# A hybrid SSD and pooling trunk on one core: the gate tiles of the first layer projected ahead of the scans in seven-product pairs, one convolution for prompt and sample rows, and another tail

## The chip, the cores and the metric

The kernel runs on one core of a Trainium2 chip. The metric is the device time of one execution in microseconds (us). Two times matter here: the timed runs (their median is the figure for the kernel) and one profiled execution, which left the profile that is read below. TensorE is called PE in the profile, its weight loads PEld, VectorE is DVE, ScalarE is ACT, GpSimd is POOL, and SyncE, which issues the DMAs, is SP.

## The reference

One inference step of a two-layer trunk runs over 1,024 prompt tokens of one sequence and over 8 sample sequences of 8 new tokens each, which come with states. Both layers are normed and modulated by a conditioning vector, and both add their output to x. All data are float32.

```python
# layer 0: Mamba-2 SSD
zxbcdt = h @ w_in                      # 1024 -> 2048 gates z, 4096 x/B/C, 32 dt
conv = conv_b + sum(xp[:, k:k + L] * conv_w[k] for k in range(4))   # causal, 3 rows of state ahead
xbc_act = silu(conv)
dt = softplus(dt_raw + dt_bias)
y, new_ssm = ssd_scan(xs, dt, A, Bm, Cm, ssm_prev)   # chunks of 128 tokens, 32 heads in 8 groups
gated = (y + d_skip * xs) * silu(z)
out = (groupwise_rmsnorm(gated) * norm_g) @ w_out    # 2048 -> 1024
# layer 1: causal pooling
uz = h @ w_in                          # 1024 -> 2048 u, 2048 z
pooled_g = window_mean(u_g, w) - u_g   # four channel groups, w = 2, 4, 8, 16
out = (grouped_matmul(pooled) * ch_scale * silu(z)) @ w_out
# then y = rmsnorm(x, final_norm_g); the new states are outputs too
```

## The kernel before: tiles, stages and order

Channels lie on the 128 partitions and tokens in the free dimension: 1,088 columns, of which 1,024 are the prompt and 64 the samples. A projection tile is 128 output channels. Its columns are done in three chunks (CH: 364, 364, 360). Float32 accuracy comes from two-part operands: each factor is rounded to a high part and the rest is a low part, and `mm1` (lines 158 to 163) issues three matmuls, high by high, high by low, low by high. A tile of the first layer is so 8 steps of the contraction x 3 chunks x 3 = 72 matmuls. A weight tile comes by DMA and is split by ScalarE (line 118) and VectorE (line 119).

The stages in order of time:

- `setup` and `front` load x, compute the norm and the modulated input hn (high and low parts, 8 tiles), and meanwhile the first two tiles and the 32 columns of dt. The modulation's shift reaches dt by 64 small matmuls of their own (pds).
- The first layer has 8 groups of 4 heads. A group needs 6 projection tiles in the order B, C, x, x, z, z. `proj_group` does them in units of one chunk (24 matmuls, 4 us). B, C and x tiles go through `conv_tile`: GpSimd does the first of four steps, VectorE the other three, prompt and sample columns in separate instructions, then tanh on ScalarE and a last step on VectorE. The two z tiles are gated (`proj_chunk`) and stay on the chip.
- `scan_group(g)` runs the scan of group g over 8 prompt chunks and one sample step. `ssd_layer` weaves it with the projections of group g + 1: one step of the scan, then one or two units, by a list of counts; the rest of the previous scan comes behind the first unit. The scan of group 7 is woven with the output projection (`op_units`).
- `ssd_out` finishes the output projection, norms and modulates for the second layer.
- `pool_layer` projects u and z: two pairs of tiles plainly, then 14 pairs (`fast_pairs`) with seven half-size products instead of eight. A pair of tiles with two halves of the contraction and two halves of the columns is a 2 x 2 block product; the seven products need sums of weight blocks (`w_sums`, GpSimd) and of activation blocks (`act_sums`, VectorE and ScalarE, called T1 to T4), and additions of the results on VectorE. A product is 24 matmuls of 272 columns. Then come the window sums (`u_pool`), the group matmuls (`pool_mix`) and the output projection.
- `last_part` does the last output tiles in column chunks (END: 416, 416, 256), and `done` and `scale` norm and store each chunk.

The order of instructions on each engine comes from the order of the code as priorities; a scheduler at build time may move a ready instruction ahead of an earlier one that is not ready by its own costs. Tiles come from `Slots` (31 buffers of 1,088 columns) or from pools with a fixed number of buffers: three PSUM tiles (mm) for the projections, two `raw` tiles for the convolution, two high and two low weight tiles. All DMAs are issued in order by SP.

## Time and profile before

| what | value |
|---|---|
| timed runs | 1692.45, 1697.51, 1698.06 us; median 1697.51 |
| profiled execution | 1692.15 us |
| its span, first to last instruction | 1690.4 us |
| mean granted TensorE clock | 0.993 |
| PE, PEld, DVE, ACT, POOL busy | 98, 93, 73, 43, 34% |
| HBM read, written | 160.95, 46.84 MB |

Stages of the span: the first layer's projections and scans from 70 to about 880 us, its output projection to 1030, the second layer's plain pairs to 1087, its fast pairs to 1382, the group matmuls to 1486, and the output projection and the tail to the end.

How to read the rows: in a group's row the numbers behind the bar are the busy time of the group in us, the mean ns of one instruction, and the idle time of the engine just ahead of them with what ended most of it. A matmul's own duration includes its latency, and matmuls overlap: 364 columns take about 330 ns each, but start 166 ns apart, so rates are worked out from counts in a stretch of time. For the same reason PE counts as busy in short pauses. In the timeline a row has the start, the length, the instruction, how many were merged, and in brackets how long its engine had been idle and what released it.

### The profile page before, as it was taken

To read this page: it belongs to the slowest core of one execution; us is meant where nothing else is said; L and a number is where in the kernel's file an instruction comes from. 1 tells how busy PE (TensorE), PEld (TensorE's weight loads), DVE (VectorE), ACT (ScalarE), POOL (GpSimd) and SP (SyncE) were. 2 spreads that over 40 slices of the span, in tenths; PEclk is the share of its full clock that TensorE was granted. 3 is DMA by queue.
4 is the path that set the end of the run, shared out by engine and by line. 5 is a ranking of instruction groups with operands and counts; after the bars stand their busy time and mean duration, and the time that the engine had idled before them with its cause. 6 is when DMAs were issued, how large, how long until landed. Compare 5 with 4: busy or idle time off the path is not lost.

```text
span 1690.4 us, 29827 instructions
## 1 busy us (share of the span) xinstructions
PE 1659.3 (98%) x11701; PEld 1579.5 (93%) x11701; DVE 1230.0 (73%) x2157; ACT 732.2 (43%) x1498; POOL 569.8 (34%) x600
## 2 busy tenths in 40 slices
PE   8999999999999999999999999999999999999997
PEld 6899999999999999998889998999999999999996
DVE  6776767677676767687788447988899996555546
ACT  5435554655555555656542027533333333221123
POOL 0224435353544445262320022365566630000012
PEclk9999999999999999999999999999999999999998
DMA  9222242333334142415874132133323368511102
GB/s 355 83 75 83 91 152 86 130 101 129 97 115 138 50 132 72 156 48 170 299 250 184 38 116 80 67 127 108 110 96 109 108 234 328 174 50 51 38 26 106
DMA packets 104461, 209.72 MB, mean 124 GB/s; under 512 B 16225, under 2 KB 56321, under 8 KB 104321
## 3 DMA queue, kind: packets, MB, share of 16 engines
q1 hardware_dynamic: 104320, 207.82, 35.9%
q8 instruction: 92, 1.51, 0.4%
q14 instruction: 49, 0.39, 0.1%
HBM read 160.95 MB, written 46.84 MB: 123 GB/s over the span
## 4 chain that ended last, share of the span: by engine, by line
PE 83%; DVE 9%; DMA 3%; issue 2%; ACT 2%; POOL 1%; SPq 0%; DVEq 0%; ACTq 0%; POOLq 0%
PE mm L161 19%; PE mm L162 18%; PE mm L163 18%; PE st L911 5%; PE st L909 5%; PE st L910 5%; PE y L549 2%; PE S L558 2%; DVE ws L771 2%; PE am L236 1%; PE y L553 1%; PE tr L499 1%; PE tr L495 1%; DVE xbc L325 1%; DMA ada<-adaA 1%
## 5 line engine op out<-in xcount | busy, mean ns | idle before, releaser
L161 PE MATMUL mm<-hh,wh 128*128 128x364 f32 (+1 forms) x1104 | 366.4, 332 | 0.0
L163 PE MATMUL mm<-hh,wl 128*128 128x364 f32 (+1 forms) x1104 | 363.6, 329 | 0.0
L162 PE MATMUL mm<-hl,wh 128*128 128x364 f32 (+1 forms) x1104 | 363.5, 329 | 0.0
L161 PE MATMUL mm<-gh,wh 128*128 128x364 f32 (+3 forms) x768 | 253.6, 330 | 3.7 <-DVE gs L698 2.6
L163 PE MATMUL mm<-gh,wl 128*128 128x364 f32 (+3 forms) x768 | 253.4, 330 | 0.0
L162 PE MATMUL mm<-gl,wh 128*128 128x364 f32 (+3 forms) x768 | 252.8, 329 | 0.0
L118 ACT ACTIVATE wh<-wr 128x1024 fp32r<-128x1024 f32 (+1 forms) x97 | 95.8, 987 | 284.1 <-PE mm L162 260.3
L695 DVE SCALAR_TENSOR_TENSOR x<-mm,gat,x 128x364 f32<-128x364 f32 (+3 forms) x192 | 108.9, 571 | 146.5 <-PE mm L163 145.9
L161 PEld LDWEIGHTS mm<-hh,wh 128*128 128x128 f32 x1104 | 208.1, 188 | 4.0 <-issue 2.8
L162 PEld LDWEIGHTS mm<-hl,wh 128*128 128x128 f32 x1104 | 208.0, 188 | 1.3 <-issue 1.0
L163 PEld LDWEIGHTS mm<-hh,wl 128*128 128x128 f32 x1104 | 207.9, 188 | 0.8 <-issue 0.4
L325 DVE SCALAR_TENSOR_TENSOR xbc<-raw,cwh,xbc 128x1024 f32<-128x1024 f32 x96 | 138.8, 1446 | 31.0 <-POOL xbc L322 31.0
L161 PEld LDWEIGHTS mm<-gh,wh 128*128 128x128 f32 x768 | 144.9, 189 | 6.6 <-issue 3.6
L163 PEld LDWEIGHTS mm<-gh,wl 128*128 128x128 f32 x768 | 144.9, 189 | 0.7 <-issue 0.5
L162 PEld LDWEIGHTS mm<-gl,wh 128*128 128x128 f32 x768 | 144.8, 189 | 0.7 <-issue 0.6
L711 POOL TENSOR_TENSOR ss<-ss,sq 128x364 f32<-128x364 f32 (+1 forms) x24 | 25.7, 1070 | 352.7 <-ACT sq L710 352.7
L911 PE MATMUL st<-hh,w 128*128 128x272 f32 x448 | 129.3, 289 | 0.0
L909 PE MATMUL st<-hh,w 128*128 128x272 f32 x448 | 129.1, 288 | 0.0
L910 PE MATMUL st<-hl,w 128*128 128x272 f32 x448 | 128.8, 288 | 0.0
L534 POOL TENSOR_TENSOR ea<-xbc,ea 128x512 f32<-128x512 f32 x56 | 83.1, 1484 | 119.7 <-ACT ea L493 112.3
L119 DVE TENSOR_TENSOR wl<-wr,wh 128x1024 fp32r<-128x1024 f32 (+1 forms) x97 | 110.9, 1143 | 13.7 <-ACT wh L118 13.3
L506 ACT ACTIVATE M<-acb,tkac 128x128 f32<-128x128 f32 x256 | 91.9, 393 | 25.9 <-PE y L549 25.2
(279 smaller groups left out, 3890.3 us busy)
## 6 DMA issues: line engine op xcount, KB each, us to landing
wr<-win SPq DMA_DIRECT2D x48, 512.0 KB, 4.1
acb<-acd SPq DMA_DIRECT2D x64, 256.0 KB, 3.7
wr<-pin SPq DMA_DIRECT2D x32, 512.0 KB, 3.7
x<-xT SPq DMA_DIRECT2D x16, 544.0 KB, 7.7
gyd<-xbc SPq DMA_DIRECT2D x16, 544.0 KB, 2.7
gr<-gyd SPq DMA_DIRECT2D x16, 544.0 KB, 6.8
zgd<-pz SPq DMA_DIRECT2D x16, 544.0 KB, 2.7
pld<-pl SPq DMA_DIRECT2D x16, 544.0 KB, 2.8
```

The source lines that it names most:

```text
L118: self.nc.scalar.activation(hi[:, :nk, :], raw[:, :nk, :], AF.Copy)
L119: self.nc.vector.tensor_tensor(out=lo[:, :nk, :], in0=raw[:, :nk, :], in1=hi[:, :nk, :].bitcast(F32), op=ALU.subtract)
L161: nc.tensor.matmul(ps[:, :n], hi[:, k, :], ah[:, a:a + n], start=first, stop=False)
L162: nc.tensor.matmul(ps[:, :n], hi[:, k, :], al[:, a:a + n], start=False, stop=False)
L163: nc.tensor.matmul(ps[:, :n], lo[:, k, :], ah[:, a:a + n], start=False, stop=last)
L325: nc.vector.scalar_tensor_tensor(out=dst[:, :NP], in0=raw[:, k:k + NP], scalar=w[k], in1=dst[:, :NP], op0=ALU.mult, op1=ALU.add)
L506: nc.scalar.activation(M[:L, r, :L], acb[:L, r, :], AF.Relu, bias=tk["ac", cc][:L, col + r:col + r + 1], scale=-1.0)
L534: nc.gpsimd.tensor_tensor(out=ea, in0=C[:, tok].unsqueeze(1).to_broadcast([P, 4, 128]), in1=ea, op=ALU.mult)
L695: nc.vector.scalar_tensor_tensor(out=x[d][:, a:a + pn], in0=ps[:, :pn], scalar=self.gat[l][:, d, 8:9], in1=x[d][:, a:a + pn], op0=ALU.mult ...
L909: nc.tensor.matmul(ps[c][:, :QUART], hi[:, k], xh[:, t], start=(k == 0), stop=False)
L910: nc.tensor.matmul(ps[c][:, :QUART], hi[:, k], xl[:, t], start=False, stop=False)
L911: nc.tensor.matmul(ps[c][:, :QUART], lo[:, k], xh[:, t], start=False, stop=(k == 3))
```

## The change

- The gate (z) tiles of all groups are projected ahead of the scans. Tiles 0 and 1 (group 0's gates) run in the front beside the modulation, in place of B and C; tiles of group 1 follow plainly; the twelve others, in six pairs, and group 0's B, C pair and x pair go through seven products (`FRONT`, `front_pairs`, `fast_pair`). The activation sums are made from x (`act_sums_front`), which therefore gets the shift added by one more pass of ScalarE; dt is then computed from that x, and the pds matmuls go. T1 overwrites half of hn, which is stored to DRAM (`b12d`) first and loaded back after the last product that needs T1.
- Each gate tile is stored to DRAM (`zsd`) and loaded again in the scan of its group, at chunk 6 (`load_z`).
- The groups' projections from group 1 on are four tiles (12 units); the weave has one unit a step.
- The convolution runs over 1,112 contiguous columns that hold prompt and sample rows with their states. Its first step is on ScalarE, with an accumulator of its own; `raw` has three buffers. The last step is split in two.
- The scan's small tiles lie in a pool that takes the place of the front's pool. There are 30 slots, 4 more in the front, and 7 wide ones later.
- The second layer takes its channel groups in the order of windows 4, 8, 16, 2, and loads and splits its group weights two tiles at a time.
- In the tail the norm of a chunk comes behind one or two units of the next chunk, the last chunk's squares are all summed by TensorE, the reciprocal root is written to PSUM too and read there by VectorE, and the shares of GpSimd and the order of the stores are others.

The core of the diff (`product`, the 24 matmuls of one product, is the old inner function of `fast_pairs` made a method; `fast_pairs` now calls `fast_pair`):

```diff
-WINDOWS = (2, 4, 8, 16)
+GROUPS = (1, 2, 3, 0)
+WINDOWS = tuple(2 << g for g in GROUPS)
...
-PK = (0, 2)
-OUT = (((0, 1), (2, 3), (4, 5), (6, 7)), ((0, 1), (2, 3), (4, 5), (6, 7)), ((0, 1), (2, 3, 4), (5, 6, 7)))
-NSLOT_A = 31
-NSLOT_B = 6
+PK = (2, 4, 3)
+OUT = (((0, 1), (2, 3), (4, 5), (6, 7)), ((0, 1), (2, 3), (4, 5), (6, 7)), ((5, 6, 7), (3, 4), (0, 1, 2)))
+NSLOT_A = 30
+NSLOT_B = 7
+NSLOT_E = 4
+FRONT = (("z", 2), ("z", 3), ("z", 4), ("z", 5), ("b", 0), ("z", 6), ("x", 0), ("z", 7))
...
+            nc.scalar.activation(t[:, :pn], t[:, :pn], AF.Identity, bias=sh)
...
     def conv_tile(self, ti, raw, dst, ncv):
-        nc = self.nc
+        nc, n = self.nc, 1112
         rv = raw[:, 1027:1115].rearrange("p (b w) -> p b w", w=11)
-        dv = dst[:, NP:TOK].rearrange("p (b i) -> p b i", i=8)
         w = [self.cwh[:, 4 * ti + k:4 * ti + k + 1] for k in range(4)]
-        b = self.cwh[:, 128 + ti:129 + ti]
-        nc.gpsimd.tensor_scalar(dst[:, :NP], raw[:, 0:NP], w[0], b, op0=ALU.mult, op1=ALU.add)
-        nc.gpsimd.tensor_scalar(dv, rv[:, :, 0:8], w[0], b, op0=ALU.mult, op1=ALU.add)
+        acc = self.raw_tile()
+        nc.scalar.activation(acc[:, :n], raw[:, :n], AF.Identity, bias=self.cwh[:, 128 + ti:129 + ti], scale=w[0])
         for k in range(1, 4):
-            nc.vector.scalar_tensor_tensor(out=dst[:, :NP], in0=raw[:, k:k + NP], scalar=w[k], in1=dst[:, :NP], op0=ALU.mult, op1=ALU.add)
-            nc.vector.scalar_tensor_tensor(out=dv, in0=rv[:, :, k:k + 8], scalar=w[k], in1=dv, op0=ALU.mult, op1=ALU.add)
+            nc.vector.scalar_tensor_tensor(out=acc[:, :n], in0=raw[:, k:k + n], scalar=w[k], in1=acc[:, :n], op0=ALU.mult, op1=ALU.add)
         nc.gpsimd.tensor_copy(ncv[:, 0:1, :], raw[:, 1024:1027].unsqueeze(1))
         nc.gpsimd.tensor_copy(ncv[:, 1:9, :], rv[:, :, 8:11])
-        th = raw[:, :TOK]
-        nc.scalar.activation(th, dst, AF.Tanh)
-        nc.vector.scalar_tensor_tensor(out=dst, in0=th, scalar=1.0, in1=dst, op0=ALU.add, op1=ALU.mult)
+        nc.scalar.activation(raw[:, :n], acc[:, :n], AF.Tanh)
+        nc.vector.scalar_tensor_tensor(out=dst[:, :NP], in0=raw[:, :NP], scalar=1.0, in1=acc[:, :NP], op0=ALU.add, op1=ALU.mult)
+        th, v = (t[:, 1027:1115].rearrange("p (b w) -> p b w", w=11)[:, :, 0:8] for t in (raw, acc))
+        nc.vector.scalar_tensor_tensor(out=dst[:, NP:TOK].rearrange("p (b i) -> p b i", i=8), in0=th, scalar=1.0, in1=v, op0=ALU.add, op1=ALU.mult)
+    def raw_tile(self):
+        return self.gp.tile([P, 1115], F32, tag="raw", bufs=3, name=self.name("raw"))
...
+    def gate_chunk(self, dst, c, ps):
+        self.z_chunk(dst, ps[:, :CH[c][1]], *CH[c])
+    def gate_store(self, i, dst):
+        self.nc.sync.dma_start(self.zsd[i], dst)
+        self.slots.free(dst)
...
+        def load_z():
+            for q in range(2):
+                zs.append(self.slots.get("z"))
+                nc.sync.dma_start(zs[q], self.zsd[2 * g + q])
...
+            if c == 6:
+                load_z()
...
+        self.last_sq = []
         for c, (a, n) in enumerate(chunks):
             for w, d in zip(ws, range(8 - nt, 8)):
+                if l and c and d == 8 - nt + c:
+                    done(c - 1)
                 self.op_unit(l, x, d, w, acts, (a, n))
                 if l == 0:
                     nc.sync.dma_start(self.x1d[d][:, a:a + n], x[d][:, a:a + n])
-                if l and c == 2 and d == 7:
-                    t = self.mt.tile([P, 416], F32, tag="mt", bufs=2, name=self.name("sq"))
+                if l and c == 2:
+                    t = self.slots.get("sq")
                     nc.scalar.activation(t[:, :n], x[d][:, a:a + n], AF.Square)
-                    self.last_sq = t
+                    self.last_sq.append(t)
                 else:
                     self.sq_add(ss, x[d], d, False, a, n, nc.vector)
                 if c == 2 and d % 2 and nt == 4:
                     self.stream_split(self.wpos + d // 2 - 2)
-            done(c)
+            if l == 0 or c == 2:
+                done(c)
...
+    def fast_pair(self, u, z, after):
+        nc, product = self.nc, self.product
+        def add(out, x, y):
+            nc.vector.tensor_tensor(out=out, in0=x, in1=y, op=ALU.add)
+        def put(dst, half, c, x, y):
+            t, o, rv = dst
+            o += HALF * half + QUART * c
+            n = QUART - NS if rv is not None and half and c else QUART
+            add(t[:, o:o + n], x[:, :n], y[:, :n])
+            if n < QUART:
+                add(rv, *(v[:, n:].rearrange("p (b i) -> p b i", i=8) for v in (x, y)))
+        cs = [slice(QUART * c, QUART * c + QUART) for c in range(2)]
+        s = self.tp.tile([P, HALF], F32, tag="mt2", bufs=2, name=self.name("u2"))
+        z1 = z[0][:, z[1]:z[1] + HALF]
+        ps = product(("mm", "mm"), "B11")
+        for c in range(2):
+            nc.scalar.activation(s[:, cs[c]], ps[c], AF.Copy)
+        after("B11")
+        ps = product(("tr", "tr"), "B21")
+        for c in range(2):
+            put(u, 0, c, ps[c], s[:, cs[c]])
+        after("B21")
+        ps = product(("y", "y"), "T2")
+        for c in range(2):
+            add(s[:, cs[c]], ps[c], s[:, cs[c]])
+        after("T2")
+        ps = product(("mm", "S"), "T3")
+        for c in range(2):
+            add(z1[:, cs[c]], ps[c], s[:, cs[c]])
+        after("T3")
+        ps = product(("mm", "mm"), "T1")
+        for c in range(2):
+            add(s[:, cs[c]], ps[c], s[:, cs[c]])
+            put(z, 1, c, ps[c], z1[:, cs[c]])
+            after(f"z1{c}")
+        after("T1")
+        ps = product(("tr", "tr"), "T4")
+        for c in range(2):
+            put(z, 0, c, ps[c], z1[:, cs[c]])
+            after(f"z0{c}")
+        after("T4")
+        ps = product(("y", "y"), "B22")
+        for c in range(2):
+            put(u, 1, c, ps[c], s[:, cs[c]])
+        after("B22")
...
         items = []
-        for g in range(8):
-            for ii in range(6):
+        items += [(io["win"][i], 8) for i in (4, 5, 10, 11)]
+        items += [(io["win"][6 * g + {"b": 0, "x": 2, "z": 4}[kind] + i], 0) for kind, g in FRONT for i in range(2)]
+        for g in range(1, 8):
+            for ii in range(4):
...
-        pds = self.pp.tile([P, 512], F32, tag="tr", bufs=2, name="pds")
-        for k in range(8):
-            for j in range(4):
-                nc.tensor.matmul(pds[32 * j:32 * j + 32, :9], wdt[:, k, :], self.shf[0][:, k, :], start=k == 0, stop=k == 7, tile_position=(0, 32 * j))
         sl.free(rst, wdts, *self.wslots)
-        dt = self.dt_phase(pdt, pds)
+        dt = self.dt_phase(pdt)
         next(dt)
         for i in range(2):
+            dst = sl.get("z")
             for c in range(3):
-                self.proj_chunk(G, i, c, pst[i][c])
-        for i, _ in enumerate(self.proj_group(G, 2)):
-            if i > 5:
-                next(dt, None)
+                self.gate_chunk(dst, c, pst[i][c])
+            self.gate_store(i, dst)
+        ops = self.act_sums_front()
+        for i in range(2):
+            w, dst = self.stream_next(), sl.get("z")
+            for c, ch in enumerate(CH):
+                ps = self.mm_tile()
+                self.mm3(ps, w, self.hn, ch)
+                self.gate_chunk(dst, c, ps)
+                next(ops)
+            self.gate_store(2 + i, dst)
+        self.front_pairs(ops, dt)
...
+    def act_sums_front(self):
+        nc, sl, x = self.nc, self.slots, self.xs
+        h1, h2 = slice(0, HALF), slice(HALF, TOK)
+        self.T = {}
+        def sub(out, x, y):
+            nc.vector.tensor_tensor(out=out, in0=x, in1=y, op=ALU.subtract)
+        def split(x, hi, lo):
+            nc.scalar.activation(hi, x, AF.Copy)
+            nc.vector.tensor_tensor(out=lo, in0=x, in1=hi.bitcast(F32), op=ALU.subtract)
+        def new(i, k, x):
+            self.T[i, k] = t = sl.get("t", F32R, extra=i < 4)
+            split(x, t[:, h1], t[:, h2])
+        for k in range(4):
+            p, r = x[k], x[k + 4]
+            sub(p[:, h1], p[:, h2], p[:, h1])
+            sub(p[:, h2], r[:, h2], p[:, h2])
+            sub(r[:, h2], r[:, h2], p[:, h1])
+            new(2, k, r[:, h2])
+            for i in range(2):
+                nc.sync.dma_start(self.b12d[2 * k + i], self.hn[k][i][:, h2].bitcast(F32))
+            yield
+        for k in range(4):
+            new(3, k, x[k][:, h2])
+            if k % 2:
+                yield
+        for k in range(4):
+            split(x[k][:, h1], self.hn[k][0][:, h2], self.hn[k][1][:, h2])
+            sl.free(x[k])
+        yield
+        for k in range(4):
+            r = x[k + 4]
+            sub(r[:, h1], r[:, h1], r[:, h2])
+            new(4, k, r[:, h1])
+            sl.free(r)
+        yield
+    def front_pairs(self, ops, dt):
+        nc, sl = self.nc, self.slots
+        self.fast_init(len(FRONT))
+        G = None
+        for n, (kind, g) in enumerate(FRONT):
+            if kind == "z":
+                ts = [sl.get("z") for _ in range(2)]
+                outs = [(t, 0, None) for t in ts]
+            else:
+                G = G or self.proj_open(g)
+                ii = 2 * (kind == "x")
+                ts = [self.proj_begin(G, ii + i) for i in range(2)]
+                outs = [(t, 3, t[:, 1027:1115].rearrange("p (b w) -> p b w", w=11)[:, :, 3:11]) for t in ts]
+            def after(x):
+                if kind == "z" and x[0] == "z":
+                    a = HALF * int(x[1]) + QUART * int(x[2])
+                    self.z_chunk(ts[1], ts[1][:, a:a + QUART], a, QUART)
+                elif kind == "z" and x in ("B21", "B22"):
+                    for c in range(2):
+                        a = HALF * (x == "B22") + QUART * c
+                        self.z_chunk(ts[0], ts[0][:, a:a + QUART], a, QUART)
+                    if x == "B22":
+                        self.gate_store(2 * g, ts[0])
+                elif kind == "z" and x == "T4":
+                    self.gate_store(2 * g + 1, ts[1])
+                if kind != "z" and x == "B22":
+                    for i in range(2):
+                        self.proj_end(G, ii + i, ts[i])
+                if n == 0 and x in ("B11", "B21"):
+                    next(ops)
+                if 0 < n < 3 and x in ("B21", "T3", "T4"):
+                    next(dt, None)
+                if n == len(FRONT) - 1:
+                    if x in ("T2", "T3"):
+                        sl.free(*[self.T[int(x[1]), k] for k in range(4)])
+                    elif x == "T1":
+                        for k in range(4):
+                            for i in range(2):
+                                nc.sync.dma_start(self.hn[k][i][:, HALF:].bitcast(F32), self.b12d[2 * k + i])
+            self.fast_pair(*outs, after)
+        sl.free(*[self.T[4, k] for k in range(4)])
...
-                self.weave(itertools.islice(sc, 11), pr, (1, 2, 2, 2, 2, 2, 2, 2, 1, 1, 1))
+                self.weave(itertools.islice(sc, 11), pr, (1, 1, 1, 1, 1, 1, 1, 1, 1, 1, 2))
...
-        self.weave(itertools.islice(sc, 10), itertools.islice(pr, 15), (1, 2, 2, 2, 2, 2, 1, 1, 1, 1), False)
+        self.weave(itertools.islice(sc, 10), itertools.islice(pr, 10), (1,), False)
...
-                self.ms_log(ss, rst, a, n, 1.0 / 1024, 0, more=self.last_sq if c == 2 else None)
+                ps = self.ms_log(ss, rst, a, n, 1.0 / 1024, 0, more=self.last_sq if c == 2 else None)
+                nc.scalar.activation(ps[:, :n], rst[:, a:a + n], AF.Exp, scale=-0.5)
                 self.rstd(rst[:, a:a + n])
-            if c:
-                scale(c - 1)
+            norms.append(ps)
+            if c == 0:
+                scale(0)
             if c == 2:
-                scale(c)
+                scale(1)
+                scale(2)
+        norms = []
```

244 lines of the change are left out of this document (108 added, 136 removed).

## The prediction

> **What bounds the kernel now.** I read the page first, then the windows by stage, the groups of instructions, the waits of TensorE, and the timeline around its longest stall in the scans.
>
> ```profile
> span 1690.4 us, 29827 instructions
> PE 1659.3 (98%) x11701; PEld 1579.5 (93%) x11701; DVE 1230.0 (73%) x2157; ACT 732.2 (43%) x1498; POOL 569.8 (34%) x600
> PE 83%; DVE 9%; DMA 3%; issue 2%; ACT 2%; POOL 1%; SPq 0%; DVEq 0%; ACTq 0%; POOLq 0%
> ```
>
> The matmuls fill the span and carry 83% of the chain that ended last, so only fewer or cheaper matmuls, or the removal of TensorE's few idle stretches, can shorten it. How full the other engines are in each stage says what can take TensorE's place. The next answer has, for each stretch, busy time and count of each engine, then clock, DMA share and GB/s.
>
> ```profile
> core 0: us, PE busy (x) PEld busy (x) DVE busy (x) ACT busy (x) POOL busy (x), PEclk, DMA share, GB/s
> 40.00:60.00 20.00, 20.00 (x174) 16.07 (x173) 15.26 (x34) 8.17 (x14) 0.00 (x0) 1.00 0.36 123
> 340.19:437.74 97.55, 97.55 (x723) 90.78 (x726) 69.56 (x125) 54.29 (x128) 43.41 (x50) 1.00 0.34 113
> 773.00:776.00 3.00, 3.00 (x17) 2.72 (x17) 1.01 (x1) 2.61 (x7) 0.32 (x1) 0.61 0.22 91
> 840.00:880.00 40.00, 40.00 (x344) 33.74 (x343) 37.24 (x72) 20.71 (x42) 10.01 (x7) 1.00 0.72 248
> 1030.00:1087.00 57.00, 53.42 (x311) 50.91 (x310) 54.22 (x108) 40.18 (x91) 13.41 (x23) 1.00 0.13 41
> 1100.00:1380.00 280.00, 280.00 (x2233) 279.97 (x2232) 247.89 (x396) 90.41 (x173) 166.48 (x131) 1.00 0.34 117
> 1382.00:1486.00 104.00, 100.22 (x601) 99.11 (x600) 68.64 (x99) 34.22 (x40) 2.16 (x2) 1.00 0.68 245
> 1500.00:1640.00 140.00, 140.00 (x845) 140.00 (x845) 69.48 (x137) 22.42 (x22) 1.93 (x2) 1.00 0.12 41
> ```
>
> One group of the first layer (a scan woven with the next group's six projection tiles) takes 97.55 us, and TensorE has no gap in it. The second layer's seven-product pairs (1100 to 1380) keep TensorE full although VectorE is at 89%.
>
> **The products.** Dense 364-column matmuls take 140/845 = 0.166 us each, the 272-column ones of a seven-product pair 280/2233 = 0.1254 us. A plain pair of tiles is 2 x 24 x 3 = 144 matmuls, 23.9 us; a fast pair is 7 x 24 = 168, 21.1 us. Eight pairs change form, six of gates and two of group 0's B, C and x: 8 x 2.8 = **-22.7 us**. This is the main term. The Trainium skill ("TensorE: Matmul & The Clock Gate", Back-to-back issue gap) gives N/2.4 + 2.5 ns; by it the eight pairs would save about 21 us, an estimate from that page. The two rows are 8% dearer, and they decide.
>
> **The front.** The 64 small pds matmuls go. The modulate gets one more ScalarE pass over 1,024 columns for each of eight tiles, because x must now hold the shifted value for the sums; it is like the pass of L303.
>
> ```profile
> 69.54 0.80 PE L1117 MATMUL pds<-shf,wdt 128*32 128x9 f32 x64
> L303 ACT ACTIVATE hh<-x,shf 128x1024 fp32r<-128x1024 f32 (+2 forms) x10 | 9.7, 977 | 12.3 <-DVE x L297 12.3
> L833 DVE TENSOR_TENSOR x<-x 128x544 f32<-128x544 f32 x8 | 5.7, 726 | 0.0
> L837 DVE TENSOR_TENSOR t<-x,t 128x544 fp32r<-128x544 f32 x12 | 10.6, 907 | 1.2 <-ACT t L836 1.2
> ```
>
> The first is **-0.8 us**. The second is 8 us of ScalarE in a stage where it is busy 8.17 of 20: zero (0 to +1). The activation sums are 16 subtractions of 0.73 and 16 splits of 0.91 us, 26 us of VectorE, beside two plain gate tiles (23.9 us of TensorE) and the first pair (21.1). Their nearest row is 1030 to 1087, where the same sums lie beside four plain tiles and TensorE idled 3.6 us; there VectorE also modulated, here it has not that work. I take **+1** (0 to +4).
>
> A pair's own VectorE work, by the rows below: 14 additions of 0.40, five weight splits of 0.88 on average, eight gates of 0.44: 13.5 us in 21.1. A pair of B, C or x tiles has two convolutions (6.5 us each, by the rows of the next part) in place of the gates and comes to 23 us, but a gate pair follows each, so the average is 18 in 21. The two bursts of some 13 us are new to this stage; the weight splits run three products (9 us) ahead, so each burst can cost up to 4. I take **+1** (0 to +8).
>
> ```profile
> L915 DVE TENSOR_TENSOR u<-st,u 128x272 f32<-128x272 f32 (+2 forms) x126 | 46.6, 400 | 8.5 <-PE st L911 7.5
> L155 DVE TENSOR_TENSOR w<-sw,w 128x512 fp32r<-128x512 f32 x42 | 41.2, 981 | 1.0 <-ACT w L153 0.3
> L155 DVE TENSOR_TENSOR w<-wr,w 128x512 fp32r<-128x512 f32 x28 | 20.6, 735 | 1.4 <-ACT w L153 1.4
> L791 DVE SCALAR_TENSOR_TENSOR pz<-zt,pz 128x272 f32<-128x272 f32 x56 | 24.5, 440 | 13.8 <-ACT zt L790 13.8
> ```
>
> **The scans.** A group loses two tiles (23.9 us of TensorE), so its period should fall from 97.55 to 73.6 us (the tiles are paid in the front; no saving beyond the products). The cover over the scan's own chain shrinks: one unit of 4 us a step instead of two. The work of the other engines a group:
>
> ```profile
> L325 DVE SCALAR_TENSOR_TENSOR xbc<-raw,cwh,xbc 128x1024 f32<-128x1024 f32 x96 | 138.8, 1446 | 31.0 <-POOL xbc L322 31.0
> L119 DVE TENSOR_TENSOR wl<-wr,wh 128x1024 fp32r<-128x1024 f32 (+1 forms) x97 | 110.9, 1143 | 13.7 <-ACT wh L118 13.3
> L322 POOL TENSOR_SCALAR xbc<-raw,cwh 128x1024 f32<-128x1024 f32 x32 | 52.3, 1635 | 143.8 <-ACT raw L353 102.6 <-ACT raw L355 41.2
> L331 DVE SCALAR_TENSOR_TENSOR xbc<-raw,xbc 128x1088 f32<-128x1088 f32 x32 | 44.4, 1388 | 6.8 <-ACT raw L330 6.8
> L323 POOL TENSOR_SCALAR xbc<-raw,cwh 128x64 f32<-128x64 f32 x32 | 44.2, 1381 | 0.0
> L326 DVE SCALAR_TENSOR_TENSOR xbc<-raw,cwh,xbc 128x64 f32<-128x64 f32 x96 | 41.5, 433 | 4.0
> L330 ACT ACTIVATE raw<-xbc 128x1088 f32<-128x1088 f32 x32 | 35.7, 1116 | 53.6 <-DVE xbc L326 53.5
> L365 DVE SCALAR_TENSOR_TENSOR z<-zt,mm 128x364 f32<-128x364 f32 (+1 forms) x48 | 25.1, 523 | 4.4 <-ACT zt L364 4.4
> L364 ACT ACTIVATE zt<-mm 128x364 f32<-128x364 f32 (+1 forms) x48 | 22.1, 461 | 20.5 <-PE mm L163 20.5
> L118 ACT ACTIVATE wh<-wr 128x1024 fp32r<-128x1024 f32 (+1 forms) x97 | 95.8, 987 | 284.1 <-PE mm L162 260.3 <-DMA wr<-pgrp 11.5 <-issue 9.7
> ```
>
> VectorE: minus 6 gates (3.1), 2 weight splits (2.3), 12 sample steps (5.2); plus 9% on 12 main steps (1.5) and a split last step (1.4): 69.6 - 7.7 = 62 us, 84% of 73.6. ScalarE gains four passes of 1.12 and loses six gate passes of 0.46 and two splits of 0.99: 54 us, 73%. GpSimd loses 4 x 3.0: 31 us. None is full. The nearest row for such a pace is 840 to 880, where the last scan runs on 4 us of output projection a step, with VectorE at 93% and no gap of TensorE. Against it stands one place where the first layer already ran one unit a step with convolutions:
>
> ```profile
> 766.42 1.44 POOL L323 TENSOR_SCALAR xbc<-raw,cwh 128x64 f32<-128x64 f32 x1
> 766.48 1.28 DVE L325 SCALAR_TENSOR_TENSOR xbc<-raw,cwh,xbc 128x1024 f32<-128x1024 f32 x1 [1.52 <-POOL xbc L322]
> 771.63 0.60 DVE L539 SCALAR_TENSOR_TENSOR xbc<-xbc,vec,y 128x128 f32<-128x128 f32 x2
> 772.03 0.79 PE L549 MATMUL y<-M,dt 128*64 128x128 f32 x8 [1.62 <-DVE xbc L539]
> 774.80 0.51 PE L163 MATMUL mm<-hh,wl 128*128 128x364 f32 x1
> 775.11 0.51 PE L161 MATMUL mm<-hh,wh 128*128 128x364 f32 x1
> ```
>
> VectorE stood 1.52 us for GpSimd's first convolution step; the scan's evacuation (L539) waited behind the convolution, and TensorE behind that, 1.62 us. Afterwards the matmuls started 0.31 us apart instead of 0.166, at a granted clock of 0.61 in that window: some 16 matmuls, another 2.2 us. So one such stall costs 3.9. The change takes the head of this stall away (GpSimd's steps go to ScalarE), but leaves the queue behind three convolution steps. Bounds: 0 to +3.9 a group; I take +0.6, nearer the gapless row: **+4** for seven groups (0 to +27). The skill's page just named (The HAM clock gate) has the clock fall only after an idle window of about 3.4 us. Here it fell after 1.6, so the row decides; by the page the stall would be 1.6 us.
>
> After the last projection tile no gate tile covers its convolution: its chain is 1.1 on ScalarE, 3 x 1.6 on VectorE, 1.1 for tanh and 1.3 for the last step, with the evacuation about 9 us, then VectorE's split of the output projection's inputs. The rest of the scan before and one modulation block cover, as I estimate from a step of 6 us, 6 of it: **+3** (0 to +9). The same convolution at the other six group ends is covered by three units (12 us) of the next tile, which need nothing from it.
>
> **DMAs.** Sixteen gate tiles go out and come back on SP's queue. The loads wait for free slots and stand ahead of the next decay rows (acb); they are asked for three steps (18 us) before use, and a load of their size lands in 6.8 us (first row below). With DMA busy 0.34 in the groups I take zero (0 to +3 in the last scan, where it is 0.72). The eight restores of hn wait for the last T1 product and are needed after two products and one chunk (10 us): zero (0 to +3).
>
> ```profile
> gr<-gyd SPq DMA_DIRECT2D x16, 544.0 KB, 6.8
> 1674.22 0.94 PE L275 MATMUL ms<-ss,ones 128*128 128x416 f32 x2 [1.34 <-DVE gs L698]
> 1680.71 0.70 PE L275 MATMUL ms<-ss,ones 128*128 128x256 f32 x2 [2.45 <-DVE ss L711]
> ```
>
> **Pool and tail.** TensorE idles 3.8 us in 1382 to 1486, behind the 16-wide window sums of the last group and the small group-weight loads. The last group now has window 2, and the loads are paired: **-3** (-5 to 0). In the tail the second norm moves behind two units (the 1.34 goes), and the last squares go straight to TensorE; of 2.45 I take 0.7, since the last evacuation and square stay: **-2** (-4 to +1).
>
> **Sum.** -22.7 - 0.8 + 1 + 1 + 4 + 3 - 3 - 2 = -19.5 us. The profiled execution took 1692.15 us, 1.75 more than its span; the timed runs 1692.45, 1697.51 and 1698.06. The difference is taken from the median: 1697.5 - 19.5 = **1678 us**.
>
> **Rivals.** (1) Nothing is lost in scans and front and both end stages gain their bounds: 1697.5 - 22.7 - 0.8 - 5 - 4 = 1665. For it: the gapless rows at 89 and 93% of VectorE. (2) The fast pairs of the front are VectorE's: the sums cost 4 and the two bursts 8, 10 more than taken: 1688. For it: 23 us of work in a 21 us pair; against it: 18 on average. (3) The other side: in the scans VectorE's in-order queue becomes the bound, the scan's evacuation stands behind each tile's three convolution steps. At 3.9 us a stall, one a group costs 27 instead of 4: 1701; two a group 1729. It outweighs everything from six stalls on. For it: the stall at 772; against it: its head was GpSimd's step, which goes. The skill ("TensorE: Matmul & The Clock Gate", Architectural detail) says that VectorE and ScalarE are strictly first in, first out; L539 behind L325 above agrees.
>
> **How the numbers follow.** About 0.3% (5 us) is what a measurement can tell from no change. Forecast 0.50 (by its bounds 1670 to 1692, nearly all faster), rival 1 0.20, rival 2 0.12 (two thirds faster), rival 3 0.18 (a third within 5 us, the rest slower). Faster 0.74, same 0.14, slower 0.12. The range, 1662 to 1700, leaves out most of rival 3 and takes in the lower bounds of rival 1.
>
> **What would show it.** Right: 272-column products before the scans at 0.125 us, scan groups of 73 to 75 us with TensorE full and VectorE near 62 busy, no gap at pool entry. Wrong: groups over 77 us with TensorE waiting for L539 or the convolution at a clock below 1, or gaps before T2 to T4 products in the front.

## The result, and the profile after

The changed kernel takes 1718.17 us (median of 4 runs, 1716.46 to 1719.48) against 1695.08 for the kernel before on the same chip (4 runs, 1692.45 to 1698.06). The ratio is 1.0139, with an interval of 1.0124 to 1.0154: it is 1.4% slower, where 1.1% faster had been forecast. The profiled execution took 1718.03 us. These are the three lines of its page that answer to the first three of the prediction:

```profile
span 1715.9 us, 30587 instructions
PE 1660.4 (97%) x11835; PEld 1562.7 (91%) x11835; DVE 1303.0 (76%) x2262; ACT 806.1 (47%) x1603; POOL 591.8 (34%) x587
PE 32%; issue 8%; POOL 8%; DVE 7%; DMA 1%; ACT 1%; POOLq 0%; SPq 0%; ACTq 0%; DVEq 0%
```

TensorE is nearly as busy as before and VectorE only three points more. The chain that ended last is no measure here: in the changed kernel it is traced back only to 732.6 us, so its shares sum to 57% and hold none of the groups before that, and the 32% can't be set against the 83% before. TensorE now waits often, for short times, in many places. The windows by stage (columns as in the prediction) say where; first the changed kernel, then the kernel before in the matching stretches.

```profile
96.80:269.90 173.10, 171.29 (x1365) 170.15 (x1364) 132.01 (x239) 69.88 (x131) 70.38 (x65) 1.00 0.29 102
...
402.20:436.00 33.80, 33.80 (x238) 30.98 (x238) 25.10 (x37) 21.67 (x45) 12.46 (x14) 1.00 0.54 177
436.00:513.70 77.70, 76.14 (x576) 66.89 (x576) 63.34 (x109) 54.19 (x124) 37.52 (x43) 1.00 0.45 143
744.00:831.60 87.60, 79.60 (x545) 66.42 (x544) 74.13 (x116) 61.02 (x131) 38.21 (x41) 0.94 0.49 166
900.00:930.00 30.00, 22.17 (x119) 21.41 (x118) 24.71 (x32) 10.88 (x11) 0.96 (x4) 0.89 0.82 299
1113.50:1412.50 299.00, 295.98 (x2355) 295.12 (x2354) 271.72 (x426) 99.44 (x192) 178.28 (x135) 1.00 0.37 129
1412.50:1508.30 95.80, 95.59 (x576) 95.21 (x575) 57.08 (x79) 24.83 (x25) 2.76 (x2) 1.00 0.63 230
```

```profile
298.20:319.80 21.60, 21.60 (x155) 19.77 (x154) 16.36 (x28) 14.20 (x33) 7.97 (x5) 1.00 0.47 161
705.00:809.10 104.10, 101.43 (x711) 91.94 (x710) 79.29 (x131) 60.31 (x134) 40.91 (x46) 0.98 0.43 136
877.00:907.00 30.00, 27.41 (x160) 26.31 (x159) 26.94 (x40) 12.24 (x12) 0.11 (x1) 0.94 0.88 318
...
1086.80:1382.00 295.20, 295.20 (x2354) 295.17 (x2353) 261.85 (x418) 97.58 (x188) 172.88 (x135) 1.00 0.35 121
1382.00:1482.00 100.00, 96.22 (x576) 95.11 (x575) 64.94 (x95) 30.22 (x36) 2.16 (x2) 1.00 0.71 255
```

The eight pairs in the front take 173.1 us, 21.6 each, close to the 21.1 of the second layer. A middle group takes 77.7 us at a clock of 1.00 with 1.56 us of idle time of TensorE (short pauses count as busy), where 73.6 was expected. VectorE's 63.3 us and ScalarE's 54.2 are close to the 62 and 54 that the prediction summed; GpSimd has 37.5 instead of 31. The stretch from scan 6 to scan 7 (744 to 831.6, before 705 to 809.1) shrank by 16.5 us only, with TensorE idle for 8 us of it. Behind the last scan TensorE idles 7.8 of 30 us (before 2.6). The second layer's pairs are 3.8 us longer, its group matmuls 4.2 shorter.

The period of a group, from the first state product (S) of one scan to that of the next, is the measure in all that follows. The starts are rounded to 0.1 us. The number of projection matmuls between the two (in the last column with those of the output projection) comes from the same rows of the trace.

| scan | 0 | 1 | 2 | 3 | 4 | 5 | 6 |
|---|---|---|---|---|---|---|---|
| before, us | 95.8 | 97.6 | 97.5 | 97.6 | 95.9 | 94.2 | 104.1 |
| after, us | 83.3 | 77.8 | 77.7 | 77.8 | 76.5 | 76.0 | 87.6 |
| fewer matmuls | 105 | 144 | 144 | 144 | 144 | 144 | 165 |

990 fewer matmuls of 0.1667 us are 165 us of TensorE; the time fell by 126.0. So **39 us were lost in the scans**: 5.0 in scan 0, 4.2 in each of the next three, 4.6 and 5.8 in scans 4 and 5, 11 in scan 6. The waits of TensorE in the whole changed kernel name the partners (us in total, times, longest):

```profile
PE mm L168 <- DVE gs L711: 6.7, 1, 6.7
PE S L569 <- POOL xl L535: 6.0, 8, 2.1
PE st L928 <- POOL w L162: 4.0, 4, 1.8
PE S L569 <- DVE Bl L531: 3.3, 6, 0.6
...
PE mm L169 <- DVE gl L696: 2.2, 2, 1.9
...
PE y L560 <- DVE M L521: 2.1, 8, 0.9
```

In a middle group of the kernel before this view is empty. In the middle group of 436 to 513.7 it lists four waits:

```profile
PE S L569 <- DVE Bl L531: 0.6, 1, 0.6
PE S L569 <- POOL xl L535: 0.4, 1, 0.4
PE tr L506 <- DVE Bl L531: 0.3, 1, 0.3
PE y L560 <- DVE M L521: 0.2, 1, 0.2
```

They sum to 1.5 of the 4.2 us that the group lost; the rest isn't listed (PE counts as busy in short pauses). Two groups of instructions of VectorE there and a piece of the timeline show one of the waits as it arises.

```profile
L334 DVE SCALAR_TENSOR_TENSOR raw<-raw,cwh,raw 128x1112 f32<-128x1112 f32 x12 | 19.6, 1633 | 0.7 <-ACT raw L332 0.6
...
L338 DVE SCALAR_TENSOR_TENSOR xbc<-raw,raw 128x1024 f32<-128x1024 f32 x4 | 4.9, 1215 | 1.3 <-ACT raw L337 1.3
```

```profile
450.79 1.72 POOL L545 TENSOR_TENSOR ea<-xbc,ea 128x512 f32<-128x512 f32 x1
...
451.30 2.38 DVE L334 SCALAR_TENSOR_TENSOR raw<-raw,cwh,raw 128x1112 f32<-128x1112 f32 x1
...
453.60 0.28 DVE L531 TENSOR_TENSOR Bl<-tr,Bh 128x128 fp32r<-128x128 f32 x1
...
453.93 0.39 PE L569 MATMUL S<-xm,Bl 128*128 128x256 f32 x1 [0.55 <-DVE Bl L531]
```

A convolution step of 2.38 us (1.36 at 220.50, where no GpSimd instruction runs beside it) stood in VectorE's queue; Bl, 0.28 us of work that the state product needs, stood behind it; TensorE waited 0.55.

### The profile page after: what moved, and what is told of

It reads as the page before. It is cut to its first block, busy times and chain, and to the rows that moved or that the text cites. A ratio compares the mean times of both kernels' runs of the same rounds, so it can differ in the third digit from the quotient of the medians.

```text
span 1715.9 us, 30587 instructions
## 1 busy us (share of the span) xinstructions
PE 1660.4 (97%) x11835; PEld 1562.7 (91%) x11835; DVE 1303.0 (76%) x2262; ACT 806.1 (47%) x1603; POOL 591.8 (34%) x587
## 4 chain that ended last, share of the span: by engine, by line
PE 32%; issue 8%; POOL 8%; DVE 7%; DMA 1%; ACT 1%; POOLq 0%; SPq 0%; ACTq 0%; DVEq 0%
PE mm L168 8%; PE mm L169 8%; PE mm L170 8%; POOL w L162 2%; PE st L928 1%; PE st L927 1%; PE st L926 1%; POOL sw L891 1%; POOL sw L892 1%; DVE gl L696 1%; DVE raw L334 1%; POOL npl L781 1%; POOL wr L896 1%; DMA rs<-rsd 1%; POOL npl L782 1%
## 5 line engine op out<-in xcount | busy, mean ns | idle before, releaser
L168 PE MATMUL mm<-hh,wh 128*128 128x364 f32 x720 | 241.3, 335 | 0.8 <-DVE z L808 0.8
L169 PE MATMUL mm<-hl,wh 128*128 128x364 f32 x720 | 240.4, 334 | 0.0
L170 PE MATMUL mm<-hh,wl 128*128 128x364 f32 x720 | 237.7, 330 | 0.0
L708 DVE SCALAR_TENSOR_TENSOR x<-mm,gat,x 128x364 f32<-128x364 f32 (+3 forms) x192 | 108.9, 571 | 154.1 <-PE mm L170 153.5
L928 PE MATMUL st<-hh,w 128*128 128x272 f32 x704 | 203.4, 289 | 0.0
L927 PE MATMUL st<-hl,w 128*128 128x272 f32 x704 | 203.3, 289 | 0.0
L926 PE MATMUL st<-hh,w 128*128 128x272 f32 x704 | 203.1, 288 | 0.0
L125 ACT ACTIVATE wh<-wr 128x1024 fp32r<-128x1024 f32 x73 | 77.2, 1057 | 243.4 <-PE mm L169 222.7
L334 DVE SCALAR_TENSOR_TENSOR raw<-raw,cwh,raw 128x1112 f32<-128x1112 f32 x96 | 155.8, 1623 | 10.1 <-ACT raw L332 9.5
L928 PE MATMUL st<-t,w 128*128 128x272 f32 x528 | 152.4, 289 | 4.8 <-POOL w L162 4.0
L927 PE MATMUL st<-t,w 128*128 128x272 f32 x528 | 151.9, 288 | 0.0
L926 PE MATMUL st<-t,w 128*128 128x272 f32 x528 | 151.8, 288 | 0.0
L169 PEld LDWEIGHTS mm<-hl,wh 128*128 128x128 f32 x720 | 136.0, 189 | 7.6 <-issue 7.3
L168 PEld LDWEIGHTS mm<-hh,wh 128*128 128x128 f32 x720 | 135.8, 189 | 6.3 <-issue 4.0
```

The lines of the kernel that those rows point to most:

```text
L125: self.nc.scalar.activation(hi[:, :nk, :], raw[:, :nk, :], AF.Copy)
L168: nc.tensor.matmul(ps[:, :n], hi[:, k, :], ah[:, a:a + n], start=first, stop=False)
L169: nc.tensor.matmul(ps[:, :n], hi[:, k, :], al[:, a:a + n], start=False, stop=False)
L170: nc.tensor.matmul(ps[:, :n], lo[:, k, :], ah[:, a:a + n], start=False, stop=last)
L334: nc.vector.scalar_tensor_tensor(out=acc[:, :n], in0=raw[:, k:k + n], scalar=w[k], in1=acc[:, :n], op0=ALU.mult, op1=ALU.add)
L708: nc.vector.scalar_tensor_tensor(out=x[d][:, a:a + pn], in0=ps[:, :pn], scalar=self.gat[l][:, d, 8:9], in1=x[d][:, a:a + pn], op0=ALU.mult ...
```

## The experiments

Three theories stood against each other. **Border**: the gates had covered the convolution of the last projected tile at the group's end; without them the next scan starts late. The steps bear this out at first sight: in 402.2 to 436 TensorE runs 159 projection matmuls without a scan step (96 in 298.2 to 319.8 before), and the next three scan steps then have 6, 5 and 22 matmuls beside them instead of 24 each. **VectorE's queue**: wherever the convolution falls, its long steps stand ahead of the scan's short ones, and one unit a step no longer hides that; this is the mechanism of the third rival. **Others**: the gate transfers, or the new convolution itself.

**The border alone.** Group 1's B tile is projected in scan 0 too, and each later scan projects the B tile of the group after next, so that three units stand behind the last convolution.

```diff
-            G = self.proj_open(g + 1)
-            sc, pr = self.scan_group(g, T), self.late(self.proj_group(G), 1, sc)
+            units = itertools.islice(every, 15 if g == 0 else 9 if g == 6 else 12)
+            sc, pr = self.scan_group(g, T), self.late(units, 1, sc)
```

> The changed kernel with its projections shifted by one tile: group 1's B tile is projected in scan 0 as well (15 units there, two in each of the first three steps), every later scan projects the last three tiles of the next group and the B tile of the one after, scan 6 has 9 units left. No work is added or left out. Theory (border): the first scan step of a group waits for the convolution of the tile that was projected just ahead of it, TensorE spends some 2.6 units early and the first three steps then have no cover; with another tile's three units behind the last convolution the four middle groups should fall from 77.8 to 73.5 to 74.5 us and the whole by 15 to 25 us, to about 1698. Rival (thin cover): one unit a step is too little in every step; the groups stay at 77 to 78 us and the whole within 4 us of 1718. Rival (GpSimd): the waits for xl stay because GpSimd is slow; the groups fall by less than 1.5 us.

1719.33 us; ratio to before 1.0137 (1.0119 to 1.0155). The border was mended: in groups 1 to 3 no step has fewer than 23 matmuls beside it any more, and the last stretch has 120. But groups 1 to 3 take 77.2, 78.7 and 78.7 us, and the whole is no faster, where 15 to 25 us had been expected. The small waits are gone, and one larger one a group stands in their place (TensorE's waits in 441.1 to 519.8, then the timeline):

```profile
PE y L560 <- DVE xbc L550: 2.3, 1, 2.3
```

```profile
465.86 1.28 ACT L337 ACT_TABLE_LOAD   x1
...
467.15 1.14 ACT L337 ACTIVATE raw<-raw 128x1112 f32<-128x1112 f32 x1
...
468.32 1.22 DVE L338 SCALAR_TENSOR_TENSOR xbc<-raw,raw 128x1024 f32<-128x1024 f32 x1 [0.47 <-ACT raw L337]
...
468.88 1.79 POOL L545 TENSOR_TENSOR ea<-xbc,ea 128x512 f32<-128x512 f32 x1 [3.58 <-ACT ea L504]
...
469.46 1.29 DVE L340 SCALAR_TENSOR_TENSOR xbc<-raw,raw 128x64 f32<-128x64 f32 x1
```

ScalarE loaded the table for tanh, the convolution's last step stood at the head of VectorE's queue for that tanh, its second part was slowed by GpSimd, and the evacuation of y (L550) that TensorE needed came behind all of it. Behind this wait the granted clock was 0.50 for 3.4 us (the window 471.5 to 474.9), which is 1.7 us more. The border theory falls as the whole cause. The times are those of the thin-cover rival, but "in every step" falls too, since two or three steps of each group now run at 6.1 us, which is 24 matmuls and the scan's own work without a wait.

**Without the convolution's steps on VectorE**, on the changed kernel.

```diff
-        for k in range(1, 4):
-            nc.vector.scalar_tensor_tensor(out=acc[:, :n], in0=raw[:, k:k + n], scalar=w[k], in1=acc[:, :n], op0=ALU.mult, op1=ALU.add)
```

> The changed kernel without the three VectorE steps of each convolution (the first step on ScalarE, tanh and the last step stay), so taps are left out of the result and some 20 us of VectorE a group go; TensorE's work is the same. Theory (VectorE's queue): the scan's small VectorE work (Bl, M, the evacuation) stands behind convolution steps of 1.4 to 2.4 us, and with one unit a step TensorE runs dry meanwhile; the middle groups should fall from 77.8 to 73 to 74.5 us. Rival (the scan's own chain over ScalarE and GpSimd is too long for one unit a step): they stay above 76. Both the shifted tile and this can't be told apart at the border alone, so the waits inside the group are to be read: those for Bl and M must go.

1691.92 us (one run), 26 less. The waits for Bl and M went, one for xl (0.5) stayed. The middle groups fell by 2.4 us, to 75.3, between the 74.5 of the theory and the 76 of the rival: the steps are more than half of the loss. The border is still there (134 matmuls without a scan step, then a step with 10). Scan 0 gained 6.1 and scan 6 4.2.

**Without the gate loads.**

```diff
-                nc.sync.dma_start(zs[q], self.zsd[2 * g + q])
```

> The changed kernel without the 16 loads of gate tiles in the scans; the gating multiplies by the y tile itself, so gates are left out of the result. Theory (border): the middle groups stay at 77.8 us within 0.3. Rival (DMA: the gate loads hold up the decay rows and the weights behind them): the groups fall by 2 us or more, and the whole by 14 us or more.

1718.08 us (one run); the middle groups take 77.7 us, as with the loads. The loads cost nothing. The stores of the gate tiles, ahead of the scans, stayed in this run and weren't tested.

**The new convolution alone, on the kernel before** (short of space, it has 30 slots, and `st` shares a buffer with `xl`), and **the kernel before with 30 slots**:

```diff
-NSLOT_A = 31
+NSLOT_A = 30
```

> The kernel before with the new convolution alone (30 slots and a shared buffer for st, to make room for the third raw buffer). Theory (border): gate tiles still cover it, TensorE stays full, the middle groups stay at 97.55 us within 0.5, the whole within 5 us of 1695, the stall at 772 us perhaps less (down to -4). Rival (the convolution itself): its passes on ScalarE and the longer chain delay the scan; the groups grow by 1 us or more each, the whole by 7 us or more.

> The kernel before with 30 slots instead of 31 and nothing else. The changed kernel and the run with the new convolution alone (30 slots each) both showed a stall of 6 to 7 us and one of 1.4 behind scan 7, where the kernel before had one of 2.9. Theory (slots): the loads of the last y tiles (gr) wait for a free slot; then this kernel shows the same two stalls, its stretch from scan 7 to the second layer is 227 to 229 us instead of 223.5, and the whole is 3 to 6 us slower than before. Rival (the convolution or the order of the queues): the stretch stays at 223.5 within 0.7 and the whole within 2 us.

The convolution alone: 1694.36 us, ratio 0.9995 (0.9982 to 1.0007). The slots alone: 1704.32 us, ratio 1.0058 (1.0045 to 1.0072). So one slot of 31 costs 0.6%, and the convolution, measured against the kernel with as many slots, gains about 10 us. With it the middle groups take 97.3 us, and the stretch from scan 6 to scan 7 98.8 against 104.1: the stall at 772 that the prediction quoted is gone. Where the missing slot acts is seen behind scan 7 (a window and TensorE's waits of the kernel with 30 slots; before, the same 30 us have TensorE busy for 27.41 us and one wait of 2.6):

```profile
877.00:907.00 30.00, 22.24 (x123) 20.62 (x123) 24.31 (x34) 10.87 (x11) 0.13 (x2) 0.91 0.93 321
```

```profile
PE mm L161 <- DVE gs L698: 5.9, 1, 5.9
PE mm L161 <- ACT gh L682: 1.9, 1, 1.9
```

These are the two stalls of the changed kernel in 900 to 930. The stretch from scan 7 to the second layer takes 230.7 us with 30 slots, 223.5 with 31, 227.4 in the changed kernel. I had expected 3 to 6 us for the slot; it was 9. In SP's queue the loads of y tiles (gr) wait for the splits (gl) that free such a tile: with 30 slots three times, 7.5 us in 860 to 910, with 31 once, 5.7 us in 860 to 905. Which of these waits decides isn't settled.

**The old convolution in the changed kernel.**

> The changed kernel with the convolution of the kernel before (first step on GpSimd, prompt and sample columns apart). Theory (VectorE's queue): 12 small VectorE steps of 0.43 us and eight GpSimd steps a group come back, and GpSimd's steps slow VectorE's beside them; middle groups 79 us or more, the whole 8 us or more above 1718. Rival (the new convolution's passes on ScalarE are what holds up the scan): groups fall below 77 us.

1791.41 us (one run). A middle group takes 87.2 us, with 4.2 us of waits for the evacuation behind the convolution. Under thin cover the old convolution would have cost 73 us more than the new one; the prediction was right that the new one helps.

**The old order of the windows in the second layer** (`GROUPS = (0, 1, 2, 3)`, loads still paired).

> The changed kernel with its channel groups in the old order of windows 2, 4, 8, 16 (loads still paired). If the order made the second layer's pairs dearer (GpSimd's small copies and weight splits beside more window sums of VectorE), the 14 pairs fall from 298.9 back to 295.2 us and their four new waits go; the pool entry then gives back what the order had gained there, up to 4 us. Rival: the pairs' waits come from elsewhere; the pairs stay at 298.9 and the whole grows by the 2 to 4 us of the pool entry. The first layer should not move by either.

1722.91 us, ratio 1.016 (1.0139 to 1.0181). The windows of the pairs and of the group matmuls:

```profile
1113.40:1408.70 295.30, 294.55 (x2349) 294.32 (x2348) 260.27 (x413) 96.16 (x185) 175.56 (x135) 1.00 0.35 122
1408.70:1511.20 102.50, 97.69 (x577) 96.56 (x576) 65.15 (x91) 28.60 (x29) 2.75 (x2) 0.98 0.66 245
```

Beside the 299.0 and 95.8 of the changed kernel: the new order saves 6.7 us at the pool entry and gives 3.7 of them back in the pairs, where the wide window sums now fall (VectorE 271.7 against 260.3 us); TensorE's waits there are for GpSimd's weight splits (2.2 us in three) and one for u (0.8), with the old order one of 0.8. With the old order and the paired loads the group matmuls take 102.5 us, against 100.0 in the kernel before, so the pairing by itself shows no gain.

**The gates of groups 5 to 7 back in the scans**, five pairs in the front instead of eight.

```diff
-FRONT = (("z", 2), ("z", 3), ("z", 4), ("z", 5), ("b", 0), ("z", 6), ("x", 0), ("z", 7))
+FRONT = (("z", 2), ("z", 3), ("b", 0), ("x", 0), ("z", 4))
...
+        for i in range(2 if G["g"] > 4 else 0):
+            w, dst = self.stream_next(), self.slots.get("z")
```

> The changed kernel with the gate tiles of groups 5, 6 and 7 back in the scans (plain, kept on the chip, weave counts of the kernel before there), five pairs in the front instead of eight. Theory (each pair taken out of a scan saves 2.8 us of products and costs that scan 4 us or more of waits): the scans that project groups 5 and 6 take 95.9 and 94.2 us again, the one that projects group 7 takes 99 to 104, with next to no waits, while the front is 65 us shorter; the whole is 1700 to 1708. Rival (the loss belongs to the new convolution or the gate transfers, not to the missing cover): the three scans keep 4 us of waits each and take 100 us or more; the whole is 1720 or more.

1702.16 us, ratio 1.0045 (1.0029 to 1.0061). The three scans take 90.9, 94.0 and 99.3 us; the first of them has 39 matmuls fewer beside it than in the kernel before. A scan with no gates beside it and one with them, in the same run:

```profile
451.90:529.60 77.70, 76.12 (x576) 66.88 (x575) 63.06 (x109) 53.84 (x124) 37.64 (x43) 1.00 0.45 143
620.50:714.50 94.00, 94.00 (x680) 88.86 (x678) 68.07 (x113) 58.71 (x129) 35.20 (x42) 1.00 0.33 101
```

With the gates TensorE is full and waits for nothing; without them the loss is the same as in the changed kernel. Each of these pairs saved at most 2.8 us of products and cost its scan more.

**The order of the queue.** The three runs that follow leave the work alone and hand it out in another order, on top of the shifted tile. First, the convolution spread over the following three units:

```diff
             nc.vector.scalar_tensor_tensor(out=acc[:, :n], in0=raw[:, k:k + n], scalar=w[k], in1=acc[:, :n], op0=ALU.mult, op1=ALU.add)
+            if k < 3:
+                yield
...
         nc.scalar.activation(raw[:, :n], acc[:, :n], AF.Tanh)
+        yield
```

> The shifted tile (as in the run with projections shifted by one tile) and each convolution handed out over the following three units: first step and one VectorE step at once, one more a unit, tanh with the third, the last step a unit later. No work is added or left out. Theory (VectorE's queue): no convolution waits for tanh at the head of the queue any more and at most one step stands ahead of the scan's work; middle groups 73 to 75 us, groups 0 to 5 together 15 to 25 us less than in the changed kernel, the whole 1693 to 1706. Rival (thin cover whatever the order): groups stay at 76.5 or more and the whole above 1710.

1712.89 us, ratio 1.0098 (1.0083 to 1.0113): a miss, with the times of the rival. Three steps in a row now take 6.1 us each (458.25 to 476.59), but the middle groups stay at 77.0. Two waits are left in a group: the sample product 1.6 us behind the convolution's last step, which stands for tanh, and the next scan's transposes 0.9 behind the last convolution.

> The spread convolutions, and group 7's two gate tiles projected plainly in the last of the scans that projects, behind its x tiles, as in the kernel before (seven pairs in the front instead of eight, weave counts of before there). Products +2.8 us. Theory: the stretch from scan 6 to scan 7 had lost 18.5 us against 7.5 before because nothing covered the last convolution and the end of the scan; with six more units there its loss falls to 7 or 8; so the whole is 5 to 9 us under the run with spread convolutions. Rival: the stretch is held by the chain behind the last scan and not by cover; the whole is 1 to 4 us above that run.

1701.12 us, ratio 1.0027 (1.0015 to 1.004): 12 less than the run before, more than the 5 to 9 expected. From the start of scan 6 to the end this kernel takes 982.1 us with 24 us more of units there, the run before 967.6: 9.5 us of the gain lie there, where the last convolution had nothing behind it.

Second, over two units (`if k == 1: yield`), so that tanh has a unit of its own before the last step:

> The run with spread convolutions and group 7's gates in the scans, with the convolution handed out over two units instead of three: first step and one VectorE step at once, the other two and tanh a unit later, the last step a unit after that. Nothing is added or left out. In the run before, the last step stood at the head of VectorE's queue for tanh and the sample product (Z) waited 1.7 us behind it, and the next scan's transposes another 1.1 us. Theory (VectorE's queue stands for tanh): both waits go, the middle groups fall from 77 to 74 to 75 us, the whole from 1701 to 1688 to 1695. Rival (it only moves the wait, since two steps now stand together): the groups stay at 76 to 77.5 and the whole at 1698 to 1704.

1693.14 us, ratio 0.999 (0.998 to 1.0). The middle groups take 75.0 us; one wait a group is left, 0.9 us for xl, behind a table load of ScalarE. Third, that load moved:

```diff
+        tq = gp.tile([P, 1], F32, tag="tq", bufs=1, name=self.name("tq"))
+        nc.scalar.activation(tq, rs[:, :1], AF.Tanh)
```

> The run with the convolutions spread over two units, plus one tanh of a single column right behind each group's norm, so that ScalarE's table load for tanh (1.28 us) comes there and not ahead of the first convolution's tanh, where Bh, xm and with them GpSimd's xl queued behind it and TensorE waited 1.1 us in step 4 of every group. Nothing else is added or left out. Theory (in-order queues: a load at the head of ScalarE's queue is what is left of the scans' loss): step 4 falls from 7.3 to 6.1 us, the middle groups from 75.1 to 73.8 to 74.3 us, the whole from 1693 to 1684 to 1690. Rival (the load is no better placed behind the norm, where the scan's exponentials queue behind it): the groups stay at 74.8 to 75.5 us and the whole within 3 us of 1693.

A middle group in the second and in the third of these kernels:

```profile
412.60:487.60 75.00, 74.07 (x577) 66.87 (x575) 61.17 (x109) 54.17 (x123) 38.35 (x42) 1.00 0.47 148
```

```profile
485.30:559.30 74.00, 74.00 (x576) 66.83 (x574) 60.48 (x109) 54.18 (x124) 38.63 (x42) 1.00 0.46 150
```

With the same 576 matmuls as the changed kernel and VectorE at 82%, a group takes 74.0 us and TensorE has no gap in it: in the middle groups the loss was one of order, not of capacity or of too few units a step. But the whole stayed at 1693.0, where 1684 to 1690 was expected, ratio 0.9988 (0.9979 to 0.9997). Scan 6 starts 4.8 us earlier than in the run before, and the stretch from scan 6 to scan 7 grows from 87.7 to 90.9; what follows gives back the rest. From scan 6 to the second layer this kernel has 72 matmuls (12 us) fewer than the kernel before and takes 327.3 us against 327.5: all 12 are lost there. One wait of 5.6 us behind scan 7, for the output projection's evacuation, is listed; what else bounds that stretch stays open. This is the only kernel whose interval lies below 1, by little: 0.1% under the kernel before.

## Why the prediction was wrong

The step that failed is **the scans**: "Bounds: 0 to +3.9 a group; I take +0.6, nearer the gapless row: +4 for seven groups", with +3 for the end of the scans. Measured were 28 us in scans 0 to 5 and 11 in scan 6, 39 instead of 7. The third rival gave 27 for one stall a group, and it had a chance of 0.18: its mechanism, in-order queues in which the scan's short work stands behind a convolution step, is what the runs show. Its form differed. It expected one wait of 1.6 us for the evacuation and 2.2 us of half clock behind it; in the middle groups there came several waits of 0.2 to 0.6 us for Bl, xl and M at a granted clock of 1.00. The expected form came when the border alone was mended: one wait of 2.3 us for the evacuation and 3.4 us at half clock behind it (1.7 us of work), 4.0 us together.

The wrong choice was the nearest row. The 840 to 880 row had VectorE at 93% without a gap, and I read the busy share as the measure. The length of single items doesn't tell the two apart either. A split of 2.91 us stood in VectorE's queue in that gapless row (first line below, kernel before), and in the last kernel of the experiments a convolution step of 2.38 us lies in a group in which TensorE has no gap (second line):

```profile
863.19 2.91 DVE L683 SCALAR_TENSOR_TENSOR gl<-gr,vec,gh 128x1088 fp32r<-128x1088 f32 x1
505.63 2.38 DVE L334 SCALAR_TENSOR_TENSOR raw<-raw,cwh,raw 128x1112 f32<-128x1112 f32 x1
```

What the runs show is the order: with the same steps and the same 576 matmuls a group takes 77.7 or 74.0 us, by what stands ahead of the scan's short work and how many matmuls are ready beside it. The row that had a whole convolution at one unit a step was the stall at 772. The sentence that three units of the next tile cover the convolution at a group's end was right for TensorE, which ran on. What it left out is that the units spent early are missing beside the next three steps; mending that alone gained nothing, as the first experiment shows.

| term | predicted, us | measured, us | from |
|---|---|---|---|
| products, with the bursts in the front pairs | -21.7 | -18.1 | 173.1 against 8 x 23.9 |
| before the pairs (pds, shift pass, act sums) | +0.2 | +2.4 | first plain gate matmul at 72.7 against 70.3 |
| scans | +7 | +39 | 126.0 saved of 165 |
| from scan 7 to the second layer | 0 | +3.9 | 227.4 against 223.5 |
| second layer's pairs | 0 | +3.8 | the windows above |
| pool entry | -3 | -4.2 | the windows above |
| tail | -2 | -0.8 | last group matmul to end, 207.6 against 208.4 |
| sum | -19.5 | +26.0 | 25.5 between the spans; the rest is rounding and stretches between |

- **Products.** Right in kind and nearly in size; a pair is shortened by 2.3 us instead of 2.8. The second rival (10 us lost in the front) was wrong: VectorE is at 76% there, and the one listed wait is 1.8 us for a weight split of GpSimd.
- **Before the pairs.** The two plain gate tiles take 24.1 us, so the sums beside them cost next to nothing. The 2.4 us lie ahead of them: TensorE's waits for the modulated input (hh, hl) are 4.5 us in 18 to 100, before 2.2 in 18 to 80. The shift pass, for which zero was taken, stands in ScalarE's queue between these tiles; that it is the cause isn't tested.
- **DMAs.** Right for the gate loads: the run without them shows no change. For the restores of hn there is no run; TensorE's waits list none for them.
- **Scan 7 to the second layer.** The edit `NSLOT_A` was not costed at all. On the kernel before, one slot fewer brings the same two stalls and 7.2 us in this stretch. The 3.9 of the table hide as much: 18 matmuls (3.0 us) of the output projection had already run ahead of scan 7 (40 instead of 22), so 6.9 us were lost here. In the changed kernel the timeline of VectorE shows the longer one as a queue again:

```profile
913.11 3.69 DVE L691 TENSOR_TENSOR gr<-gr,rs 128x1088 f32<-128x1088 f32 x3 [0.68 <-DMA rs<-rsd]
916.72 5.13 DVE L696 SCALAR_TENSOR_TENSOR gl<-gr,vec,gh 128x1088 fp32r<-128x1088 f32 x4
921.77 0.52 DVE L708 SCALAR_TENSOR_TENSOR x<-mm,gat,x 128x296 f32<-128x296 f32 x1
```

  Seven scalings and splits, released late by a transfer, stood together ahead of the evacuation (L708, L711) that TensorE waited 6.7 us for. That the slot is its cause here too is argued from the likeness, not shown.
- **Pool.** The gain at the entry was right in size; as far as the run with the old order shows, it comes from the order of the windows and not from the paired loads. That the new order moves VectorE's wide sums in among the pairs was named by no term; it took nearly all of it.
- **Tail.** Right in sign, within its bounds.

## What to carry to other kernels

Before work is taken out of a loop because the busiest engine should get less of it, ask what that work was hiding: here 24 us of matmuls a group were the cover for queues that run in order, and a saving of 2.8 us a pair cost 4.2. Neither the busy share of an engine nor its longest single item told it here; the order of its queue did. So lay out, step by step, what stands ahead of each short instruction that TensorE waits for, and how many matmuls are ready meanwhile. Where cover is thin, another order of the same long work can win the loss back, as it did in the middle groups though not behind them, and a buffer given up elsewhere must be costed like any other edit.
